# Early weight squares: their loads issued from ScalarE's DMA queue instead of SyncE's

## The chip, the cores and the metric

The kernel runs as one launch on one core of a Trainium2 chip. The core has TensorE (PE, matrix products), VectorE (DVE), ScalarE (ACT), GpSimd (POOL) and SyncE (SP); ScalarE and SyncE can both issue DMA transfers, each from a queue of its own, and all transfers run on the core's 16 DMA engines. The metric is the device time of the launch in microseconds; the median of 3 runs of the kernel before is 2465.13 us (2464.49 to 2465.89).

## What is computed

Two transformer blocks over 512 tokens of width 1024, in float32, with 256 memory rows and 256 context rows beside them:

```
first_block:   h = rms_norm(x);  z = h @ w_in           (spatial gating, sparse attention)
               x += concat(a, b) @ w_out
               x += memory_cross_attention(rms_norm(x), mem)
               x += square(relu(rms_norm(x) @ w_ff1)) @ w_ff2        w_ff1 1024x4096
second_block:  two mixer layers; each
               z = (rms_norm(x) * (1 + scale) + shift) @ w_in         15 column parts
               window attention, latent attention, short convolution
               m = sum over 3 branches of sigmoid(g) * (y * silu(z)) @ w_branch
               x += gate * rms_norm(m @ w_o)
```

The time goes to the weight products; each weight is read from HBM once for its product.

## The kernel before

**Weight products.** A float32 weight tile is split into a high and a low half, and each product is three matmuls: high by high, high by low, low by high (L471 to L473). Early weights go as `fp32r` halves: ScalarE copies the high half (L320), VectorE subtracts to get the low half (L321). From the feed-forward part on, weights go as float16 halves, and for these a scale is needed first: the sum of squares over the whole group of weight blocks. ScalarE squares each tile of the group with an accumulator (L234), VectorE adds the sums (L483), a one-column matmul adds over the partitions (L485), and GpSimd and VectorE make the scale (L486 to L488). Then ScalarE (L327) or GpSimd (L325) writes the high half and VectorE the low half (L345).

**The weight stream.** `Stream` reads all weights in the order of use, in tiles of up to 512 KB, into buffers named `raw` (`loads`, L211). These loads are issued from SyncE's queue, in order; a load waits there until VectorE has finished with the tile that held its buffer. There are 3 buffers at first, and `more_raw` adds more.

**Early squares.** For the groups of the first feed-forward piece and of both mixer layers, the sums of squares are made ahead of time: the tile is loaded a second time into one buffer of its own (`self.slot`), squared there by ScalarE in place (`early_sum`, L272), and forgotten; the sums land in the tile `gse`. `pump` runs at every step of the program; once per interval (`every`, 5000 or 8000 ns of planned time) `early_step` squares what was loaded last and then begins the next load (L262). There is one such buffer, so at any time one early load is under way or one early square is due. There are 82 of them; they lie beside the end of the memory attention, its output product and the eight pieces of the feed-forward part (`ff1`, `ff2`). In `ff1`, ScalarE also takes each product out of PSUM (L1453, L1454); in `ff2`, VectorE does (L1301).

**Order.** The program is written in one order, and a scheduler then puts the instructions of each engine and queue in a row of its own. A row is worked off in order. So an instruction on ScalarE stands behind every ScalarE instruction ahead of it, and a load on SyncE behind every load ahead of it.

Of the kernel before, what the change touches and what calls it, by code (L numbers as in the profile page):

```python
# [184 lines left out]
class Stream:  # L185
# [67 lines left out]
    def early_step(self):  # L253
        if self.state.clk < self.next:
            return
        if self.job is not None:
            self.early_sum()
        while self.jobs:
            i = self.jobs.pop(0)
            if i >= self.nd:  # L260
                for dst, src in self.chunks[i][0]:
                    self.nc.sync.dma_start(out=dst(self.slot), in_=src)  # L262
                self.job = i
                break
        self.next = self.state.clk + self.every
# [2247 lines left out]
```

## Time and profile before

| | |
|---|---|
| median of 3 runs | 2465.13 us |
| the profiled execution | 2463.02 us, of which 2461.2 us span |
| mean granted TensorE clock | 0.972 |
| busy: PE, DVE, ACT, POOL | 2278.1, 1542.3, 1294.3, 314.4 us |
| early squares (L272), first and last start | 394.0 and 883.6 us |

In the trace, an engine's busy time is that of its compute instructions; issuing of DMAs and waiting on semaphores is not in it. "SPq" and "ACTq" are the parts of SyncE and ScalarE that issue DMAs. A bracket such as [5.19 <-ACT wh L327] says that the engine stood idle for 5.19 us ahead of this instruction and that ScalarE's write of the tile `wh` in line 327 ended it. The granted clock is a share of TensorE's full speed.

### The profile page before, as it was taken

Reading aid. Unit: us, or ns where it says so; the run is one execution under the profiler, and the core shown is the slowest. Engines: PE = TensorE matmul, PEld = TensorE weight load, DVE = VectorE, ACT = ScalarE, POOL = GpSimd, SP = SyncE. Lnnn points to the kernel's source line nnn. Section 1 sums busy time; section 2 is a strip of 40 time slices with the busy share of each in tenths; the row PEclk is TensorE's granted clock in tenths of the full one; section 3 lists DMA queues with packets and bytes.
Section 4 is the critical chain, followed back from the end, with each engine's and each line's share of the span. In section 5 each row is a group of like instructions: output and inputs, shape, how many; then the busy total and the mean of one; then the engine's idle time right before and its main releaser. Section 6 shows DMA issues by size and latency. Waiting matters only on the chain. (4 is left out here: it accounts for less than half of the span.)

```text
span 2461.2 us, 38164 instructions
## 1 busy us (share of the span) xinstructions
PE 2278.1 (93%) x14342; PEld 1511.3 (61%) x14342; DVE 1542.3 (63%) x3136; ACT 1294.3 (53%) x2705; POOL 314.4 (13%) x703
## 2 busy tenths in 40 slices
PE   7899898988989889999998899999979999999998
PEld 6777686633434355776686655666846666764446
DVE  6878677745465467765677644444478666865553
ACT  5656457756776544343567644422333445765532
POOL 4310321100010021001200000000331121000001
PEclk9899899999999999999999999999989999999999
DMA  4512446766676651111222322121242113233311
GB/s 155 137 46 74 143 137 208 252 192 187 200 231 187 188 158 43 42 38 48 83 65 71 124 84 72 61 69 61 95 129 63 49 49 104 70 96 118 103 61 60
DMA packets 224493, 267.84 MB, mean 109 GB/s; under 512 B 29868, under 2 KB 171100, under 8 KB 224308
## 3 DMA queue, kind: packets, MB, share of 16 engines
q1 hardware_dynamic: 200356, 228.83, 30.2%
q10 hardware_dynamic: 23952, 36.57, 4.4%
q8 instruction: 112, 1.84, 0.3%
q14 instruction: 73, 0.60, 0.1%
HBM read 248.49 MB, written 16.88 MB: 108 GB/s over the span
## 5 line engine op out<-in xcount | busy, mean ns | idle before, releaser
L471 PE MATMUL mm<-hTh,wh 128*128 128x512 f16 (+1 forms) x1040 | 393.6, 379 | 17.9 <-ACT wh L327 15.4
L473 PE MATMUL mm<-hTh,wl 128*128 128x512 f16 (+1 forms) x1040 | 391.7, 377 | 3.6 <-DVE wl L345 3.4
L472 PE MATMUL mm<-hTl,wh 128*128 128x512 f16 (+1 forms) x1040 | 393.4, 378 | 0.0
L345 DVE SCALAR_TENSOR_TENSOR wl<-raw,gs,wh 128x512 f16<-128x512 f32 x256 | 179.4, 748 | 144.0 <-ACT wl L234 96.4
L471 PEld LDWEIGHTS <-wh 128*128 128x128 f16 x1712 | 168.1, 98 | 160.1 <-ACT wh L327 17.4
L473 PEld LDWEIGHTS <-wl 128*128 128x128 f16 x1712 | 167.9, 98 | 149.8 <-DVE wl L345 5.5
L472 PEld LDWEIGHTS <-wh 128*128 128x128 f16 x1712 | 168.0, 98 | 143.9 <-issue 9.2
L799 ACT ACTIVATE ph<-mm 128x512 f16<-128x512 f32 (+2 forms) x300 | 146.1, 501 | 186.9 <-PE mm L795 175.9
L321 DVE TENSOR_TENSOR wl<-raw,wh 128x512 fp32r<-128x512 f32 (+2 forms) x244 | 156.8, 670 | 84.7 <-ACT wh L320 68.1
L800 DVE SCALAR_TENSOR_TENSOR pl<-mm,ph 128x512 f16<-128x512 f32 (+2 forms) x300 | 166.4, 567 | 66.2 <-ACT ph L799 63.9
L320 ACT ACTIVATE wh<-raw 128x512 fp32r<-128x512 f32 (+2 forms) x244 | 141.4, 612 | 96.4 <-PE mm L472 23.5
L471 PE MATMUL mm<-wh,hTh 128*128 128x512 f32 (+5 forms) x512 | 184.6, 362 | 6.8 <-ACT hTh L476 4.0
L473 PE MATMUL mm<-wh,hTl 128*128 128x512 f32 (+5 forms) x512 | 182.5, 357 | 1.7 <-DVE hTl L477 1.7
L472 PE MATMUL mm<-wl,hTh 128*128 128x512 f32 (+5 forms) x512 | 182.7, 358 | 0.1
L327 ACT ACTIVATE wh<-raw,gs 128x1024 f16<-128x1024 f32 x128 | 143.3, 1139 | 70.6 <-PE mm L472 63.6
L795 PE MATMUL mm<-ident,P 128*128 128x128 f32 x928 | 153.3, 282 | 6.5 <-DVE cv L1774 1.6
L272 ACT ACTIVATE raw<-raw 128x1024 f32<-128x1024 f32 (+3 forms) x82 | 83.4, 1017 | 136.1 <-DMA raw<-in_w_in_dram 127.0
L345 DVE SCALAR_TENSOR_TENSOR wl<-raw,gse,wh 128x512 f16<-128x512 f32 (+2 forms) x164 | 118.4, 767 | 47.5 <-POOL wh L325 26.0
L234 ACT ACTIVATE wl<-raw 128x1024 f16<-128x1024 f32 (+1 forms) x140 | 135.8, 970 | 19.6 <-DMA raw<-in_w_ff_dram 8.9
L325 POOL TENSOR_SCALAR wh<-raw,gse 128x1024 f16<-128x1024 f32 (+3 forms) x54 | 64.6, 1198 | 492.9 <-PE mm L472 300.4
L782 ACT ACTIVATE P<-S,s 128x768 f32<-128x768 f32 (+4 forms) x160 | 105.7, 665 | 35.2 <-PE mm L795 17.0
L795 PEld LDWEIGHTS mm<-ident,P 128*128 128x128 f32 x928 | 108.7, 145 | 20.2 <-DVE pl L800 3.0
(517 smaller groups left out, 5487.2 us busy)
## 6 DMA issues: line engine op xcount, KB each, us to landing
raw<-in_w_in_dram SPq DMA_DIRECT2D x184, 512.0 KB, 3.6
raw<-in_w_ff_dram SPq DMA_DIRECT2D x68, 512.0 KB, 5.0
raw<-in_w_mod_dram SPq DMA_DIRECT2D x48, 512.0 KB, 4.4
raw<-in_w_branch_dram SPq DMA_DIRECT2D x28, 512.0 KB, 3.4
raw<-in_w_o_dram SPq DMA_DIRECT2D x16, 512.0 KB, 3.7
raw<-in_w_in_dram SPq DMA_DIRECT2D x16, 384.0 KB, 3.2
raw<-in_cmp_w_dram SPq DMA_DIRECT2D x16, 256.0 KB, 3.5
raw<-in_w_out_dram SPq DMA_DIRECT2D x8, 512.0 KB, 4.7
```

The costliest lines, as they stand in the source:

```text
L234: nc.scalar.activation(lo[:, :b - a], t[:, a:b], AF.Square, accum_out=g.t[:, g.cols:g.cols + 1])
L320: nc.scalar.activation(hi[:, :m], src, AF.Copy)
L321: nc.vector.tensor_sub(lo[:, :m], src, hi[:, :m].bitcast(FT))
L327: nc.scalar.activation(hi[:, :m], src, AF.Copy, scale=s)
L345: self.nc.vector.scalar_tensor_tensor(l[:, b], src[:, b], s, h[:, b], op0=OP.mult, op1=OP.subtract)
L471: PE.matmul(ps, ah, bh, start=start, stop=False)
L472: PE.matmul(ps, ah, bl, start=False, stop=False)
L473: PE.matmul(ps, al, bh, start=False, stop=stop)
L782: ACT.activation(P, v[:, j, :], AF.Exp, bias=it.nb[:, j:j + 1], accum_out=it.den[:, j:j + 1])
L795: PE.transpose(ps[:, a - a0, :], it.P[0 if len(it.P) == 1 else j][:, c:c + 128], ident)
L799: ACT.activation(ph[:, :m], ps[:, :m], AF.Copy, scale=PSC)
L800: DVE.scalar_tensor_tensor(pl[:, :m], ps[:, :m], PSC, ph[:, :m], op0=OP.mult, op1=OP.subtract)
```

## The change

The second loads of the weight tiles for the early squares are begun by ScalarE instead of SyncE. Nothing else is edited:

```diff
--- before.py
+++ after.py
@@ -259,7 +259,7 @@
             i = self.jobs.pop(0)
             if i >= self.nd:
                 for dst, src in self.chunks[i][0]:
-                    self.nc.sync.dma_start(out=dst(self.slot), in_=src)
+                    self.nc.scalar.dma_start(out=dst(self.slot), in_=src)
                 self.job = i
                 break
         self.next = self.state.clk + self.every
```

The scheduler's rows move with it. On SyncE's row of before, around the weights of the fourth of the eight feed-forward pieces, the early loads (L262) stand between the loads of the stream (L211):

```order
L262 DMA raw<-in_w_in_dram 128x3x288
L211 DMA raw<-in_w_ff_dram 128x4x256 x4
L262 DMA raw<-in_w_in_dram 128x2x288
L211 DMA raw<-in_w_ff_dram 128x2x512 x2
L262 DMA raw<-in_w_in_dram 128x2x384 x3
L211 DMA raw<-in_w_ff_dram 128x2x512
L262 DMA raw<-in_w_in_dram 128x2x384
L262 DMA raw<-in_w_in_dram 128x8x128 x2
```

On the same row of the changed kernel there, only the stream is left, in the same order:

```order
L211 DMA raw<-in_w_mod_dram 128x2x512 x4
L211 DMA raw<-in_w_ff_dram 128x4x256 x4
L211 DMA raw<-in_w_ff_dram 128x2x512 x4
L211 DMA raw<-in_w_mod_dram 128x2x512 x4
L211 DMA raw<-in_w_ff_dram 128x4x256 x4
```

All 82 early loads have left SyncE's row. On ScalarE's row of before, ahead of the first high halves (L327) of the fourth piece's `ff1` weights, three squares stand in a row:

```order
L272 ACTIVATE raw,gse<-raw 128x768
L234 ACTIVATE wl,gs<-raw 128x512
L320 ACTIVATE wh<-raw 128x512
L234 ACTIVATE wl,gs<-raw 128x512
L272 ACTIVATE raw,gse<-raw 128x768 x2
L272 ACTIVATE raw,gse<-raw 128x1024
L320 ACTIVATE wh<-raw 128x512
L327 ACTIVATE wh<-raw,gs 128x1024 x2
```

On ScalarE's row of the changed kernel at the same place, the loads stand between them:

```order
L272 ACTIVATE raw,gse<-raw 128x768
L234 ACTIVATE wl,gs<-raw 128x512
L320 ACTIVATE wh<-raw 128x512
L262 DMA raw<-in_w_in_dram 128x2x384
L234 ACTIVATE wl,gs<-raw 128x512
L272 ACTIVATE raw,gse<-raw 128x768
L262 DMA raw<-in_w_in_dram 128x8x128
L272 ACTIVATE raw,gse<-raw 128x1024
L262 DMA raw<-in_w_in_dram 128x8x128
L320 ACTIVATE wh<-raw 128x512
L234 ACTIVATE wl,gs<-raw 128x1024
L327 ACTIVATE wh<-raw,gs 128x1024 x2
```

After the square of 768 columns that opens both pieces, three more squares stand ahead of the high halves before and two now; two of the loads stand right behind a square, and one behind two other instructions. The longest such distance is in the first piece of the feed-forward part, on ScalarE's row of the changed kernel:

```order
L272 ACTIVATE raw,gse<-raw 128x1024
L1453 ACTIVATE z<-mm 128x256
L476 ACTIVATE hTh<-S 128x4x128
L1454 ACTIVATE z<-z 128x256
L327 ACTIVATE wh<-raw,gs 128x1024 x4
L234 ACTIVATE wl,gs<-raw 128x1024
L262 DMA raw<-in_w_in_dram 128x4x256
L1454 ACTIVATE z<-z 128x256
L234 ACTIVATE wl,gs<-raw 128x1024
L272 ACTIVATE raw,gse<-raw 128x1024
```

Here eight instructions stand between a square and the load that follows it, and two between the load and its square; on SyncE's row nothing of ScalarE's stood ahead of the load.

## Rows read from the trace of the kernel before

**Rows 1.** Page: busy time of each engine.
```profile
PE 2278.1 (93%) x14342; PEld 1511.3 (61%) x14342; DVE 1542.3 (63%) x3136; ACT 1294.3 (53%) x2705; POOL 314.4 (13%) x703
```

**Rows 2.** Busy by stretch: us, PE, PEld, DVE, ACT, POOL, clock, DMA share, GB/s.
```profile
0.00:390.00 390.00, 355.17 (x2560) 290.21 (x2560) 287.21 (x535) 222.23 (x513) 104.35 (x271) 0.95 0.38 117
390.00:885.00 495.00, 435.17 (x2147) 217.45 (x2147) 283.07 (x569) 330.60 (x594) 33.83 (x74) 0.96 0.66 209
885.00:2461.00 1576.00, 1487.76 (x9635) 1003.61 (x9635) 972.00 (x2033) 741.44 (x1600) 176.22 (x358) 0.98 0.25 75
```

**Rows 3.** Early loads (L262): who waited (us, times), and time to landing.
```profile
  ACT raw L272: 136.0, 57
...
DMA to landing us min/median/max: 3.1/3.5/5.8
```

**Rows 4.** ScalarE's timeline, 589 to 606 us: start, us, instruction, idle before.
```profile
590.05 0.84 ACT L272 ACTIVATE raw<-raw 128x768 f32<-128x768 f32 x1 [2.87 <-DMA raw<-in_w_in_dram]
590.80 0.18 ACT L272 ACTIVATION_READ_ACCUMULATOR raw<-raw 128x1 f32 x1
...
594.14 0.84 ACT L272 ACTIVATE raw<-raw 128x768 f32<-128x768 f32 x1 [1.42 <-DMA raw<-in_w_in_dram]
...
598.36 0.85 ACT L272 ACTIVATE raw<-raw 128x768 f32<-128x768 f32 x1 [3.28 <-DMA raw<-in_w_in_dram]
...
602.93 1.06 ACT L272 ACTIVATE raw<-raw 128x1024 f32<-128x1024 f32 x1 [3.64 <-DMA raw<-in_w_in_dram]
...
604.51 2.17 ACT L327 ACTIVATE wh<-raw,gs 128x1024 f16<-128x1024 f32 x2
```

**Rows 5.** SyncE's timeline, 589 to 606 us.
```profile
591.01 0.37 SPq L262 DMA_DIRECT2D raw<-in_w_in_dram  x1
```

**Rows 6.** PE's timeline, 598 to 606 us.
```profile
605.70 0.61 PE L471 MATMUL mm<-hTh,wh 128*128 128x512 f16 x1 [5.19 <-ACT wh L327]
```

**Rows 7.** Busy by stretch, behind that wait (columns of rows 2).
```profile
606.00:614.00 8.00, 7.87 (x28) 2.94 (x27) 4.33 (x8) 7.97 (x14) 0.02 (x1) 0.75 0.76 223
```

**Rows 8.** SyncE's waits, 390 to 885 us: us in total, times, longest.
```profile
SPq L262 <- DMA raw<-in_w_in_dram: 144.2, 52, 6.2
SPq L211 <- DVE wl L345: 98.2, 50, 6.7
SPq L262 <- ACT raw L272: 79.2, 70, 3.0
```

**Rows 9.** ScalarE by line and form, 390 to 885 us: busy us, mean ns.
```profile
L327 ACT ACTIVATE wh<-raw,gs 128x1024 f16<-128x1024 f32 x60 | 65.5, 1133 | 0.0
...
L320 ACT ACTIVATE wh<-raw 128x512 fp32r<-128x512 f32 x70 | 40.2, 620 | 9.3 <-DVE oc L1299 6.3 <-DMA raw<-in_w_mod_dram 2.1 <-PE mm L1505 0.7
```

**Rows 10.** ScalarE's timeline, from 565 us, with a DMA that ScalarE issues.
```profile
565.49 0.92 ACT L272 ACTIVATE raw<-raw 128x864 f32<-128x864 f32 x1 [1.92 <-DMA raw<-in_w_in_dram]
565.63 0.39 ACTq L1525 DMA_DIRECT2D mf<-raw_d  x1
...
566.41 4.25 ACT L327 ACTIVATE wh<-raw,gs 128x1024 f16<-128x1024 f32 x4
570.57 1.65 ACT L320 ACTIVATE wh<-raw 128x512 fp32r<-128x512 f32 x3
572.13 0.57 ACT L1453 ACTIVATE z<-mm 128x512 f32<-128x512 f32 x1
```

**Rows 11.** Loads of the stream (L211), 390 to 885 us: time to landing.
```profile
DMA to landing us min/median/max: 3.3/4.7/8.4
```

**Rows 12.** The two context loads (L1565) that ScalarE issues, 512 KB each.
```profile
L1565 ACTq DMA_DIRECT2D ctx<-in_ctx_dram x2: 357/360/363, 426.6 to 697.1; - x2
...
DMA to landing us min/median/max: 4.8/5.8/6.9
```

**Rows 13.** ScalarE's waits for the stream, 390 to 885 us.
```profile
ACT wl L234 <- DMA raw<-in_w_ff_dram: 8.9, 8, 4.3
```

**Rows 14.** PE's timeline, 690 to 701 us.
```profile
699.70 0.58 PE L471 MATMUL mm<-wh,ffh 128*128 128x512 f16 x1 [3.63 <-DVE oc L1301]
```

## The prediction

> **What bounds the kernel now.** First the page's busy times: TensorE is busy for 2278.1 us of 2461.2 [rows 1]. Then the table by stretch, cut where the early squares begin and end. From 390 to 885 us TensorE is busy for 435.17 of 495 us, so it idles 59.8 us, a third of all its idle time (183 us) in a fifth of the span; DMA share is 0.66 there and 0.25 after it [rows 2]. The edit acts in that stretch.
>
> ScalarE there is busy for 330.60 us [rows 2] and stands for another 136.0 us ahead of 57 early squares, each time for the square's load [rows 3]: together 467 of 495 us. It works in order, so such a wait also holds up the high halves of the weights and the removal of products from PSUM behind it. The timeline shows one such chain. Three squares follow each other with no other work; the last starts at 602.93 after 3.64 us of waiting, the high halves (L327) start only at 604.51 [rows 4], and TensorE's next matmul has by then waited 5.19 us [rows 6]. [...]
>
> What ends these waits? The loads are not late in their queue. SyncE waits 70 times, 79.2 us in all, for a square to end [rows 8]: 1.13 us each, about one square's length with the read of its accumulator, so it was at the load already when the square began. In the chain shown, the read ends at 590.98 [rows 4] and the load is issued at 591.01 [rows 5]. The load then takes 3.5 us to land (median) [rows 3]. ScalarE waits because one buffer serves all early squares, and another queue does not change that.
>
> **The change, part by part.** All durations are from the profiled execution: 2463.02 us, 2461.2 of them span; the median of the runs is 2.1 us above it. TensorE's price for a wait on ScalarE is at most 59.8 / 136.0 = 0.44 us per us, if all its idle time in the stretch is put down to these waits; I use 0.44 and, as the other end, 0 to 1.
>
> *Moved: 82 loads in ScalarE's row.* Counting what stands between successive squares (81 pairs, each instruction at its mean duration less the 0.1 us by which it overlaps the next: L327 1.04, L320 0.52 [rows 9], the rest likewise), and a landing of 3.55 us, ScalarE's waits come to 116.6 us for the row of before (the trace has 136.0; some loads land later) and 109.9 us for the changed row, if a load is issued the moment the previous square ends. That is 6.7 us less, 2.9 us at 0.44. One place has a name: ahead of the fourth piece's `ff1` two squares stand now, three before, so its high halves come one step earlier, 602.93 - 598.36 = 4.57 us [rows 4], and most of the 5.19 us wait and the slow 2.0 us behind it go; against that, the memory attention and the second piece get longer waits by the same count. I take -4, with 0 and -13 as ends.
>
> *Is the load issued the moment the square ends?* In 48 of the 81 cases one to eight ScalarE instructions stand between the square and the next load. One row bears on it: the DMA of L1525 is issued at 565.63, while the square of 565.49 runs, with four L327, three L320 and one L1453, eight instructions ahead of it in the row, not yet begun [rows 10]. So ScalarE's issuing part can run eight compute instructions ahead of the engine, and none of the 81 distances is longer than eight. I take 109.9 us. If every load were issued only when its turn came on the engine, the same count gives 161.0 us.
> [...]
>
> *Added: 82 DMA issues on ScalarE*, 0.37 us each on SyncE [rows 5] and 0.39 us for one on ScalarE [rows 10]. Where compute work stands between the square and the load, the issue lies beside it. In 33 cases the load stands right behind the square and ScalarE has nothing to run meanwhile; in 10 of these the next square follows at once and would wait anyway. That leaves 23 x 0.39 = 9.0 us in which other work starts later; x 0.44 = +4.0. Ends: 0, if the next square waits as long less, and 9.0.
>
> *The landing.* The load now shares the DMA engines with stream loads from another queue that no longer stand behind it. Alone in its turn it lands in 3.5 us [rows 3]; stream loads take 4.7 us [rows 11], and the two context loads that ScalarE itself issued in this stretch 5.8 us (one of 4.8, one of 6.9) [rows 12]. Squares that wait are those with little ScalarE work around them, when few buffers come free and few stream loads go out, so I stay near the row of the same kind: 3.7 us. That raises the waits from 109.9 to 118.3 us; x 0.44 = +3.7. Ends: 0, and at 4.7 us a sum of 178.2, +68.3 x 0.44 = +30.
>
> *Removed: early loads in SyncE's row.* The stream is no longer behind the 144.2 + 79.2 = 223 us that SyncE spends at L262 [rows 8]. But the stream then waits for buffers (98.2 us for VectorE's low halves alone [rows 8]), and ScalarE waited only 8.9 us for a stream load, once 4.3 us [rows 13], which came with a TensorE wait of 3.63 us [rows 14]. 8.9 x 0.44 = -3.9. Ends: -8.9, and 0 if the buffers are the limit.
>
> Sum: -4 + 4.0 + 3.7 - 3.9 = -0.2 us on the profiled execution; on the median, 2465 us. All ends one way give -22 and +39.
>
> **Rivals.**
> *The loads stand in line on ScalarE.* The issuing part doesn't get ahead where an instruction in between itself waits, so the load goes out in its turn: waits of 161.0 instead of 109.9 us, +51.1 x 0.44 = +22, 2487 us. For it: 48 loads have something in between, in the worst place eight instructions with four L327. Against it: the eight ahead in rows 10. It decides from about a quarter of its size, 11 us of waits.
>
> *The two queues slow each other.* Stream loads run beside the early loads, which land in 4.7 us: +30 in place of +3.7, 2491 us. For it: the context loads [rows 12] and a DMA share of 0.66. Against it: before, stream loads followed right behind as well, and the early loads landed in 3.5. It decides from about 3.9 us.
> [...]
>
> *The freed stream pays more than I count.* Weight tiles arrive early enough for all their squares (L234) to be done sooner, the chain of squares, scale and high halves starts earlier at each piece, and waits like the 5.19 us go together with the slow clock behind them: two such places, 2 x (5.19 + 2.0) = -14, 2451 us. For it: 223 us at L262. Against it: only 8.9 us of ScalarE's waits are for stream loads.
>
> *The edit does nothing*, since the loads go out at the same moments and the buffers hold the stream as before: inside my forecast.
>
> **How the numbers follow.** Within 0.2% (4.9 us, about what a measurement of this kernel can tell from none) counts as the same. My forecast, terms that cancel, has 0.56, of which 0.37 stays within 4.9 us, 0.10 is faster and 0.09 slower, because the scheduler's rows changed all through the stretch. The freed stream has 0.19, all faster. The line on ScalarE has 0.13 and the slowed landing 0.12, both slower. Together: faster 0.29, same 0.37, slower 0.34. The range runs from 2447, beyond the faster rival, to 2490, the slower ones' size; the forecast's own is 2456 to 2475.
>
> **What would show it.** Right: ScalarE's waits at L272 stay between 105 and 145 us and the stretch from first to last square stays near 490 us; the early loads land in 3.4 to 3.9 us, 0 to 0.1 us behind the square; TensorE's 5.19 us wait shrinks and others grow. Wrong: waits over 155 us, with loads issued microseconds behind the square (the line on ScalarE) or landing in over 4 us (the queues); TensorE's idle time in the stretch under 50 us (the freed stream); or a difference outside this stretch, which I count at nothing.

## The result, and the profile after

The changed kernel takes 2477.89 us (median of 5 runs, 2472.81 to 2482.15) beside 2464.49 us of the kernel before (2460.63 to 2465.89): 1.0057 times, 95% interval 1.0040 to 1.0075. It is slower by 13 us, and no change was forecast.

Where in the program? The three stretches of rows 2 again, of the kernel after, with the middle one cut 20 us longer (the last early square starts at 909.2 us now, 883.6 before):

```profile
0.00:390.00 390.00, 351.12 (x2561) 286.43 (x2562) 288.46 (x538) 225.23 (x520) 104.25 (x271) 0.96 0.39 121
390.00:905.00 515.00, 447.68 (x2159) 223.57 (x2160) 282.17 (x569) 330.34 (x586) 38.05 (x79) 0.93 0.63 199
905.00:2476.00 1571.00, 1485.51 (x9625) 1001.39 (x9623) 970.51 (x2031) 742.29 (x1600) 174.70 (x354) 0.98 0.25 75
```

TensorE idles 67.3 us of the middle stretch (59.8 before), and its granted clock there is 0.93 (0.96 before) [rows 2]. To compare equal work I cut by matmuls from here on: from the 2500th to the 4950th matmul of TensorE's row, both counted in the traces, it is 549.8 us before and 569.6 after (+19.8). At its start the profiled run of after is 4.3 us ahead, and what lies behind it is 0.7 us shorter. The 4.3 us are no more than single profiles differ by chance (experiment 5).

The early loads of after; the columns are those of [rows 3]:

```profile
who waited for it (us, times):
  ACT raw L272: 152.2, 63
...
DMA to landing us min/median/max: 2.9/4.5/8.9
```

ScalarE waits 152.2 us and not 136.0, and the median landing is 4.5 us and not 3.5 [rows 3]. That median, over all 82 loads, is a poor sign by itself: it is 4.3 us in order_only (experiment 3), whose loads are on SyncE and for which ScalarE waits 138.5 us. SyncE's waits for the low halves in 385 to 900 us, before and then after:

```profile
SPq L211 <- DVE wl L345: 110.9, 52, 11.2
...
SPq L211 <- DVE wl L321: 48.3, 28, 7.2
```

```profile
SPq L211 <- DVE wl L345: 284.5, 72, 13.3
SPq L211 <- DVE wl L321: 144.7, 33, 14.0
```

The stream no longer stands behind early loads, but for the low halves: 284.5 us now, and 110.9 before. So a stream load goes out the moment a buffer is free, whatever the early loads are doing. Its loads land as fast as before [rows 11], and ScalarE waits for them 6.9 us, 8.9 before [rows 13]:

```profile
DMA to landing us min/median/max: 3.4/4.7/7.3
```

```profile
ACT wl L234 <- DMA raw<-in_w_ff_dram: 6.9, 7, 2.9
```

What the freed stream does to an early load is seen at 763 us, in ScalarE's row and then in SyncE's:

```profile
762.35 1.06 ACT L272 ACTIVATE raw<-raw 128x1024 f32<-128x1024 f32 x1 [0.33 <-DMA raw<-in_w_in_dram]
763.31 0.19 ACT L272 ACTIVATION_READ_ACCUMULATOR raw<-raw 128x1 f32 x1
763.53 0.46 ACTq L262 DMA_DIRECT2D raw<-in_w_in_dram  x1
769.87 1.06 ACT L272 ACTIVATE raw<-raw 128x1024 f32<-128x1024 f32 x1 [6.37 <-DMA raw<-in_w_in_dram]
```

```profile
761.46 0.37 SPq L211 DMA_DIRECT2D raw<-in_w_ff_dram  x1
763.54 0.37 SPq L211 DMA_DIRECT2D raw<-in_w_ff_dram  x1
```

One stream load began 2.1 us ahead of the early load and one beside it, and the next square, which follows with nothing in between, waits 6.37 us. Sorted over the stretch: of the early loads for which ScalarE waited over 0.3 us, those with a stream load issued in the 2.6 us ahead of them take 5.42 us from issue to square in after (36 of 60), the others 3.49. Before, they take 5.23 (23 of 55) and 3.50. The price of such company has hardly changed; its frequency has.

The fourth piece's high halves are the place that the prediction named as a gain [rows 4 and 6]. In after, two squares stand ahead of them, the last one starts at 606.84, and TensorE's longest wait there is 1.98 us, for VectorE, in place of 5.19 for the high halves, for which it now waits 0.73:

```profile
606.84 1.06 ACT L272 ACTIVATE raw<-raw 128x1024 f32<-128x1024 f32 x1 [3.57 <-DMA raw<-in_w_in_dram]
607.80 0.19 ACT L272 ACTIVATION_READ_ACCUMULATOR raw<-raw 128x1 f32 x1
608.01 0.37 ACTq L262 DMA_DIRECT2D raw<-in_w_in_dram  x1
608.49 0.63 ACT L320 ACTIVATE wh<-raw 128x512 fp32r<-128x512 f32 x1 [0.51 <-ACT raw L272]
```

```profile
609.90 0.39 PE L1506 MATMUL mm<-wl,ms 128*2 128x512 f32 x1 [1.98 <-DVE wl L321]
...
611.25 0.39 PE L471 MATMUL mm<-hTh,wh 128*128 128x512 f16 x1 [0.73 <-ACT wh L327]
```

That gain came. But the row of 608.49 shows something else: ScalarE stood for 0.51 us between a square and the next instruction, with no data to wait for. Its issuing part was then at the early load (608.01).

### The profile page after: what moved, and what is told of

The parts are those of the page before. It is cut to its first block, busy times and chain, and to the rows that moved or that the text cites. A ratio compares the mean times of both kernels' runs of the same rounds, so it can differ in the third digit from the quotient of the medians.

```text
span 2476.1 us, 38086 instructions
## 1 busy us (share of the span) xinstructions
PE 2284.3 (92%) x14342; PEld 1511.4 (61%) x14342; DVE 1541.1 (62%) x3136; ACT 1297.9 (52%) x2705; POOL 317.0 (13%) x703
## 5 line engine op out<-in xcount | busy, mean ns | idle before, releaser
L327 ACT ACTIVATE wh<-raw,gs 128x1024 f16<-128x1024 f32 x128 | 143.4, 1140 | 72.0 <-PE mm L472 63.0
L782 ACT ACTIVATE P<-S,s 128x768 f32<-128x768 f32 (+4 forms) x160 | 105.9, 665 | 34.1 <-PE mm L795 16.7
```

What stands on the lines that cost most here:

```text
L327: nc.scalar.activation(hi[:, :m], src, AF.Copy, scale=s)
L782: ACT.activation(P, v[:, j, :], AF.Exp, bias=it.nb[:, j:j + 1], accum_out=it.den[:, j:j + 1])
```

## The experiments

**Theory 1:** the queue costs. Stream loads that SyncE no longer holds share the DMA engines with the early loads, which land later. **Theory 2**, as first put: the issue on ScalarE and the new order of the rows cost, not the transfers. The runs of experiments 3 and 4 then separate order, issue and transfers. All ratios are against the kernel before in the same set of runs.

| kernel | times before, 95% interval | ScalarE idle ahead of early squares | all ScalarE idle | TensorE idle, slow clock (us), in the cut |
|---|---|---|---|---|
| before, its two profiles | 1; 0.9996 (0.9984 to 1.0007) | 136, 141 | 167, 170 | 68 and 48; 65 and 65 |
| the change, its two profiles | 1.0057 (1.0040 to 1.0075); 1.0051 (1.0037 to 1.0066) | 152, 157 | 191, 196 | 76 and 79; 80 and 72 |
| order_only | 0.9957 (0.9945 to 0.9969) | 139 | 172 | 68 and 44 |
| queue_only | 1.0140 (1.0127 to 1.0153) | 135 | 204 | 93 and 99 |
| queue_only_held | 1.0120 (1.0104 to 1.0137) | 135 | 197 | 93 and 82 |
| one_behind | 1.0084 (1.0072 to 1.0097) | 156 | 193 | 85 and 79 |
| no_late | 1.0088 (1.0071 to 1.0105) | 151 | 190 | 84 and 82 |
| pause_only | 1.0033 (1.0021 to 1.0045) | 124 | 181 | 78 and 72 |
| held | 0.9979 (0.9965 to 0.9993) | 140 | 182 | 65 and 58 |
| two_sync | 0.9801 (0.9782 to 0.9819) | 43 | 100 | 37 and 41 |
| two_scalar | 0.9858 (0.9838 to 0.9878) | 49 | 104 | 42 and 38 |

"All ScalarE idle" sums the idle time ahead of its instructions from the first early load to 9 us behind the last; "slow clock" is the time at 0.5 of full speed, the lower of the two values (1.0 and 0.5) that the clock has in the records of before and after. Both, and the idle time ahead of early squares, are worked out from one profile for each kernel (two for the first two rows); in two_sync 36 of the 43 us are waits for the load, in two_scalar 41 of 49, in the other rows all but 2 us or less.

**1. The disputed transfer by itself (pairs).** The program only does this, eight cases six times (e: early load on SyncE, a: on ScalarE, s: stream load on SyncE):

```
for case in ("s", "a", "es", "se", "sa", "ssa", "sse", "ess"):
    memset(t)                     # all loads of a case wait for it
    ... the loads of the case, in this order ...
    vector.tensor_copy(seen, early part of t);  gpsimd.tensor_copy(seen, stream parts)
```

> A kernel that leaves out the whole computation and only loads 512 KB weight tiles, in eight cases, six times each, every case after the last one has ended: an early load alone from SyncE, alone from ScalarE, an early load on SyncE with one or two stream loads behind it or ahead of it in the same queue, and an early load on ScalarE begun in the same moment as one or two stream loads on SyncE. Theory 1 (two queues share the DMA engines, one queue serves in order): alone 3.5 us from either engine; 3.5 with stream loads behind it in one queue, about 4.8 with one ahead and 6.1 with two ahead; 4.5 to 5 from ScalarE beside one, 5.5 to 6.5 beside two, and the stream load beside it is late as well. Theory 2 (ScalarE's issue is what costs): from ScalarE it lands 0.5 us or more later than from SyncE when alone, and beside stream loads no later than that.

VectorE's row, the first five cases in that order; each copy waits, from the memset, for the early load (in the first case the only load):

```profile
8.51 0.15 DVE L411 COPY seen<-t 128x1 f32<-128x1 f32 x1 [3.91 <-DMA t<-in_w_in_dram]
15.88 0.15 DVE L411 COPY seen<-t 128x1 f32<-128x1 f32 x1 [3.89 <-DMA t<-in_w_in_dram]
24.20 0.15 DVE L411 COPY seen<-t 128x1 f32<-128x1 f32 x1 [4.84 <-DMA t<-in_w_in_dram]
34.48 0.15 DVE L411 COPY seen<-t 128x1 f32<-128x1 f32 x1 [5.38 <-DMA t<-in_w_in_dram]
43.33 0.15 DVE L411 COPY seen<-t 128x1 f32<-128x1 f32 x1 [5.32 <-DMA t<-in_w_in_dram]
```

From its own issue, mean of six: alone 3.81 us from SyncE and 3.78 from ScalarE; first in one queue with another behind it 4.39; behind another 4.99; from ScalarE beside one on SyncE 5.38, beside two 5.51. ScalarE's queue is not slower by itself. Being first in a shared queue protects a load only in part, by 1.0 us against two queues. Being behind and being beside come to the same: 4.99 is less than 5.38 only because that load's own issue begins later; counted from the memset, as in the rows shown, the two are seen after 5.38 and 5.32 us. With two stream loads in the same queue, the first of the three takes 4.41 us and the last 5.99. Theory 1 had the direction, but too much protection (3.5 expected for the first in a queue).

**2. Holding the stream, and two buffers (held, two_sync, two_scalar).**

```diff
 # held: the change, and in early_sum
+            self.nc.sync.dma_start(out=self.held[:, n:n + 1], in_=g.t[0:1, g.cols:g.cols + 1])
 # two_sync, two_scalar: early_step loads first, then squares the older buffer
+                t = self.slot.pop(0)
+                    self.nc.sync.dma_start(out=dst(t), in_=src)        # two_scalar: nc.scalar
+                self.job.append((i, t))
+        if len(self.job) == 2 or (self.job and not self.jobs):
+            self.early_sum()
```

> The changed kernel, with one thing added: after each early square SyncE copies the square's sum (4 bytes, read by nobody) to memory, so its queue waits for the square as it did before, and the stream loads behind it are held until then. The early loads stay on ScalarE. Theory 1 (stream loads that are no longer held go out ahead of the early load and share the DMA engines with it): early loads that ScalarE waits for land in 3.5 to 4 us again instead of 4.5, ScalarE's waits at the early squares fall from 152 to 120 to 140 us, and the time comes back to 2463 to 2471 us; if only the order within one queue protects the early load, since stream loads still begin 0.4 us behind it in the other queue, it stays at 2472 or above. Theory 2 (issue on ScalarE, and the order of its row): nothing comes back, 2474 to 2482 us.

> The kernel before with two early buffers instead of one: each early load is begun one interval earlier, before the square of the other buffer. The stream has five buffers then, not six. Early loads on SyncE. If ScalarE's waits for the early loads are what TensorE's gaps in this stretch come from, the waits at the early squares fall from 136 to under 25 us, TensorE's idle time between the first and last early square falls from about 68 to 30 to 50 us and its slow stretches with it, and the time is 2425 to 2450 us. If the gaps have another source (the stream's buffers, VectorE's low halves), 2458 to 2475 us.

> The same two early buffers, with the early loads on ScalarE. Theory 1: where the early load has a whole interval to land, the sharing of the DMA engines is covered, so it is within 5 us of the same kernel with the loads on SyncE. Theory 2 (82 issues on ScalarE of 0.37 us and loads that wait for their turn in its row): 8 to 16 us slower than that kernel, as the change was on one buffer.

held came back to 0.9979, as Theory 1 asked; but its loads still take 5.75 us where a stream load is ahead, and the 4-byte copies had made the scheduler write other rows: ScalarE's differs from the change's in 274 of 2094 places (accumulator reads left out). So it settled nothing, except that the order had to be taken out of the comparison.

two_sync: 0.9801, 49 us saved, beyond the range that was expected. Its loads, waits and stretch:

```profile
  ACT raw L276: 36.1, 26
```

```profile
390.00:810.00 420.00, 389.65 (x1957) 197.91 (x1956) 259.58 (x530) 320.48 (x576) 29.26 (x66) 0.96 0.74 232
```

TensorE idles 30.4 of 420 us, and the last early load is begun at 799.7 us (878.1 before), with one stream buffer less. So the waits for early loads were a large part of what this stretch lost, and the remedy is a second buffer and not another queue; how much of the 49 us the new rows of two_sync give was not separated. On ScalarE's queue the same kernel is 0.6% slower (0.9858). Theory 1 expected these two within 5 us; it is 14. Their rows differ as well, so this doesn't say why.

**3. Order and queue apart (queue_only, order_only, queue_only_held, change_again).** The rows of one kernel are taken from a first building of the program and laid on the other, as links from each instruction to the next on its engine:

```
rows = rows of the scheduler with the early loads on SyncE (order_only: on ScalarE)
queue_only:  each early load moved into ScalarE's row, right behind the square that frees its buffer
order_only:  early loads taken out of ScalarE's row; SyncE's row left to the scheduler
for row in rows:
    for p, q in zip(row, row[1:]):
        tc.add_manual_dep(traced[q], traced[p].name, same, reason="row")
```

> Every engine's row is held to that of the kernel before, instruction by instruction; only the 82 early loads leave SyncE's row and stand on ScalarE's, each right behind the square that frees its buffer. So the queue changes and the order of the work does not. Theory 1 (the queue: stream loads no longer held and sharing the DMA engines): early loads that are waited for land about 0.4 us later than before, and the time is 2474 to 2482 us, as the change's. Theory 2 (the scheduler's new rows): 2462 to 2468 us, as before.

> The rows of TensorE, VectorE, GpSimd and ScalarE are those of the changed kernel, instruction by instruction, but the 82 early loads are on SyncE, where the scheduler places them between the stream loads. So the order of the work changes and the queue does not. Theory 1: 2462 to 2468 us, as before. Theory 2: 2474 to 2482 us, as the change's.

> The kernel of the rows of before with the early loads on ScalarE, and where each early load stood in SyncE's row there is now a copy of the square's sum (4 bytes, read by nobody), which waits for the same square. So the stream loads are held as before, the early loads go out at the same moment from the other queue, and the order of all compute is that of before. Theory 1 with the hold as its cause: 2462 to 2469 us. Theory 1 with the sharing as its cause (the stream load goes out 0.4 us behind the early load and takes half the DMA engines, 5.4 us to land instead of 4.4 in the pairs): 2470 to 2482. Theory 2: 2462 to 2468 us, and the same without the copies.

> The changed kernel once more, beside the others on one chip, with a second profile. Both theories: 1.003 to 1.008 times the kernel before. If the slow stretches of TensorE's clock ahead of 300 us differ between its two profiles (37.5 us in the one of before, 27.3 in the first of the change), that part of the difference is chance; if they agree, it belongs to the kernels.

Neither theory alone: the queue costs 1.40% (34.6 us) and the new order gives back 0.43% (10.6 us). With both edits the change has 1.0051, so in the changed order the queue costs 1.0051 / 0.9957, 0.94% or 23 us. Holding the stream gave 1.0120, whose interval overlaps that of 1.0140; by the medians the hold takes back 5 of the 34.6 us. Early loads with a stream load ahead became fewer (23 in place of 28), but those took 5.91 us in place of 5.57. So the lost hold is not the main cost.

queue_only has the surprise. It waits as long for early loads as before (134.9 us), and yet is the slowest. Its ScalarE row, and the same place of before:

```profile
543.13 1.06 ACT L273 ACTIVATE raw<-raw 128x1024 f32<-128x1024 f32 x1 [3.66 <-DMA raw<-in_w_in_dram]
544.09 0.19 ACT L273 ACTIVATION_READ_ACCUMULATOR raw<-raw 128x1 f32 x1
544.31 0.37 ACTq L263 DMA_DIRECT2D raw<-in_w_in_dram  x1
544.73 1.15 ACT L321 ACTIVATE wh<-raw 128x512 fp32r<-128x512 f32 x2 [0.45 <-ACT raw L273]
```

```profile
535.92 0.19 ACT L272 ACTIVATION_READ_ACCUMULATOR raw<-raw 128x1 f32 x1
536.02 1.13 ACT L320 ACTIVATE wh<-raw 128x512 fp32r<-128x512 f32 x2
```

Before, the next instruction starts with the end of the read; with the load in between, it starts 0.45 us later, because the issue first waits for the square and then takes 0.37 us while the engine has nothing. There are 63 such pauses, nearly all of 0.45 to 0.51 us, some 30 us in all. Where a square waits for its load anyway, the pause should shorten that wait: in pause_only (experiment 4), which adds pauses alone, ScalarE idles 124 us ahead of early squares in place of 136 and 141. That would hide what later landings add here.

**4. Pauses, late issues and what is left (one_behind, pause_only, no_late).**

```
one_behind:  in queue_only's ScalarE row, each load one compute instruction behind the square
no_late:     as one_behind, but 5 loads (numbers 7, 9, 26, 49, 81) right behind their square
pause_only:  rows of before; scalar.dma_start(out=sums[:, n:n+1], in_=<the square's sum>) right behind each square
```

> The kernel of the rows of before with the early loads on ScalarE, but each load stands one compute instruction behind the square that frees its buffer, and not right behind it (where the next instruction is a square again, it stays right behind). With the load right behind the square that kernel showed 63 pauses of 0.45 to 0.51 us on ScalarE between a square and the next compute instruction. If the changed queue costs through these pauses (the issue runs while the engine has nothing), they go, and the time comes back from 1.014 to 1.000 to 1.005 times the kernel before. If it costs through the sharing of the DMA engines, the time stays at 1.010 to 1.015. Both in part: 1.005 to 1.010.

> The kernel before in every row, early loads on SyncE, with one thing added: ScalarE issues a copy of the square's sum (4 bytes, read by nobody) right behind each early square, at the place where the early loads stood in the kernel that changed the queue alone. So ScalarE has the issue's pause and the early loads stay in one queue with the stream. If the pauses are the cost: about 63 of 0.5 us, 1.008 to 1.014 times the kernel before. If the sharing is the cost: 0.999 to 1.003.

> As the kernel whose early loads stand one instruction behind the square (1.0084 times before), but the five loads that were issued 0.9 to 6.2 us late there, because the instruction ahead of them in ScalarE's row was itself waiting (13.4 us in all), stand right behind their square. If these late issues are most of what that kernel still lost: 1.001 to 1.005. If the sharing of the DMA engines by two queues is: the late issues go, ScalarE's waits for early loads fall from 156 to about 143 us, and the time stays at 1.006 to 1.009.

One instruction in between takes the pauses from 63 to 1 and the time from 1.0140 to 1.0084. The pauses alone cost 0.33%; these copies are issued faster, in 0.24 us and not 0.37, and the 59 pauses are shorter:

```profile
540.77 0.24 ACTq L284 DMA_DIRECT2D sums<-gse  x1
541.05 1.15 ACT L329 ACTIVATE wh<-raw 128x512 fp32r<-128x512 f32 x2 [0.31 <-ACT raw L274]
```

So the pauses cost 0.3 to 0.6%, 8 to 14 us, in queue_only. The late issues cost nothing that can be measured (1.0088 beside 1.0084, though they fell from 13.4 to 1.1 us). What is left in no_late, 0.9% or 22 us, has the rows of before, few pauses and no late issue. By elimination, and not by a run of its own, it is put down to the traffic of two queues; ScalarE's waits for early loads are 151 us there, 10 to 15 more than before, with 27 loads that have a stream load ahead (23 and 25 in the two profiles of before) at 5.48 us each (5.23 and 5.37). Its waits for stream tiles have grown as well, to 12.4 us (8.9 and 8.1 in the two profiles of before):

```profile
ACT wl L235 <- DMA raw<-in_w_ff_dram: 12.4, 7, 6.4
```

**5. The kernel before against itself (before_again).**

> The kernel before, unchanged, beside itself, with a second profile: 0.998 to 1.002. Its ScalarE waits at the early squares within 5 us of 136, its stretch from first to last early load within 5 us of 494; differences beyond that would make the same differences between other traces chance. The slow stretches of TensorE's clock ahead of 300 us are expected to differ from 37.5 us, since kernels with equal rows there showed 20 to 41 us.

```profile
  ACT raw L272: 140.4, 59
...
DMA to landing us min/median/max: 3.1/3.6/5.7
```

0.9996, with an interval that holds 1; no other interval of the table does. A single trace is worth less: up to the 2000th matmul six profiles with the rows of before (two of before, queue_only, queue_only_held, one_behind, pause_only) have equal rows and yet show 37.5, 26.6, 33.2, 40.7, 20.5 and 34.1 us of slow clock, and lengths from 262.8 to 269.2 us. The 4.3 us ahead of the early squares in the two first traces are within that spread.

## Why the prediction was wrong

*Order, -4 (0 to -13).* It was 2.6 times that: 0.9957, -10.6 us. It did not come through ScalarE's idle time, as the step had it, which is 172 us in order_only and 167 to 170 before. The wait ahead of the fourth piece did shrink, in order_only as in the change. The slow 2.0 us that the step counts behind it are an estimate from rows 7, 8 us at a granted clock of 0.75 (8 x 0.25); that clock is 0.50 from 603.2 to 609.9 us before, and in after still 0.50 from 611.6 to 614.9 us, so about half of that slow stretch is left. Where the rest of the 10.6 us lies stays open: the one profile of order_only spans 2462.1 us, those of before 2461.2 and 2464.3, each on another chip. Nor need it be ScalarE's order alone: on SyncE's row, which was left to the scheduler, 43 of the 82 early loads stand elsewhere among the stream's loads than before.

*Loads are issued when the square ends.* Right in 75 of 81 cases, as rows 10 suggested. The other six loads were 1.1 to 2.5 us late, 11.2 us in all. Three of them stood behind an instruction that itself waited for a stream tile, for 0.38 to 1.33 us, and went out with its start; for the other three no such wait is seen right there. One of the first kind:

```profile
504.35 0.57 ACT L1453 ACTIVATE z<-mm 128x512 f32<-128x512 f32 x1
505.31 0.63 ACT L234 ACTIVATE wl<-raw 128x512 fp32r<-128x512 f32 x1 [0.38 <-DMA raw<-in_w_ff_dram]
505.32 0.37 ACTq L262 DMA_DIRECT2D raw<-in_w_in_dram  x1
```

The rival of loads standing in line exists, at a fifth of its 51 us; taking such late issues out cost or gave nothing measurable in experiment 4 (no_late beside one_behind).

*Issue pauses, 23 of 0.39 us.* In count and size nearly right for the changed kernel: 17 pauses of 0.45 to 0.51 us, some 8 us. In its row 48 of the 81 loads have an instruction in between, which queue_only has not.

*Landing, 3.7 us.* The step that failed. "Squares that wait are those with little ScalarE work around them, when few buffers come free and few stream loads go out": 36 of the 60 loads that were waited for had a stream load just ahead (24 of 59 in order_only, which has the same rows), and the mean of the 60, from issue to square, is 4.65 us in place of 4.22. The row it went by hid this: 3.5 us is the median of all 82 loads, while 23 of the 55 that were waited for had company in the trace of before already. Against order_only ScalarE's waits for early loads rose by 14 to 18 us, where this term had 8.4. The rival that the two queues slow each other, put at 0.12, is the one that the runs bear out in direction; in the change's own order the queue's 23 us are close to its +26, partly by luck, since the 17 pauses are in the 23 and not in the 26; and the order's gain hid half of it. The pairs point the same way: 3.78 us alone from ScalarE, 5.38 beside a load of SyncE.

*Freed stream, -3.9.* No steady gain is shown. ScalarE's waits for stream tiles (rows 13) went from 8.9 to 6.9 us, but with equal rows they fall in one case, from 12.2 in order_only to 6.9, and rise in the other, from 8.9 to 12.4 in no_late; SyncE now stands 284.5 us for the low halves.

*The price, 0.44 us per us of ScalarE's waits.* Too low. Against 168 us of ScalarE idle time before, the kernels with equal order give 34.6 us for +36 (queue_only), 29.6 for +29 (queue_only_held), 20.7 for +25 (one_behind), 21.7 for +22 (no_late) and 8.1 for +12 (pause_only): 0.7 to 1.0. With other rows it need not hold: two_sync gives -49 for -69, but held is 5 us faster with +14. The 0.44 shared out TensorE's idle time and left out the time of slow clock, which in the cut went from 48 and 65 us before to 79 and 72 in the change. By the means of the two profiles, TensorE's idle time there rose by 11 us, 0.46 per us of ScalarE's, and the slow clock by 19 us. In after, matmuls of 128x512 start every 0.43 us at 613 us, where the clock is 0.50, and every 0.22 us at 615 us, where it is 1.00; at that half speed the 19 us cost, by estimate, another 9.

With these: ScalarE's idle time rose by 22 to 27 us where the sum had +1.8 (-6.7 + 9.0 + 8.4 - 8.9); against order_only, which has the same rows, it rose by 19 to 23. At 0.9, a value from the middle of the prices above, that is +17 to +21, less 10.6 for the order, +6 to +10. Measured: +13; at 1.0 it would be +8 to +13. The price comes from these same runs, so this sum shows only that they fit together. The sum came to zero because a term that was too small was multiplied by a price that was too small, and set off against a gain that was too small as well.

What stays open: how much of the 0.9% in no_late is the early loads' landing and how much the stream's (ScalarE's waits grew by 10 to 15 us for the first and by some 4 for the second); and why two_scalar is 14 us behind two_sync.

## What to carry to other kernels

Where ScalarE waited for a transfer into its only buffer, another queue did not help here (queue_only 1.0140); a second buffer did, by 2% (two_sync 0.9801). A DMA that ScalarE issued right behind the square it waits for stopped the engine for 0.45 to 0.51 us, its issue (0.37 us) and some 0.1 us, 63 times in queue_only; with one instruction in between (one_behind), 1 such pause was left. And where a scheduler rewrites the rows with every edit, hold the rows and move one thing at a time: here the edit's two effects had opposite signs, 34.6 us against 10.6.

## What was not expected of the hardware

- A load of up to 512 KB that stands directly behind the square it waits for cost ScalarE 0.45 to 0.51 us, its issue (0.37 us) and some 0.1 us; a 4-byte one 0.31 to 0.37 us, with an issue of 0.24 us.
- A 512 KB load took 3.81 us alone, 4.39 with another behind it in the same queue, 4.99 behind another and 5.38 beside one from another engine's queue: order within a queue protected the first load by about 1 us and not wholly.
- Equal rows of work ran with 20.5 to 40.7 us of slow clock in their first 265 us, a spread of 6 us between single executions.
